# Attention stage of a hybrid block: TensorE's order written by the build's scheduler instead of by hand, with the value products marked urgent and taken in reverse

## The chip, the cores and the metric

The kernel runs on one core of one Trainium2 chip. The metric is the device time of one execution in microseconds (us), the median over the timed runs. The profile shows one further execution, taken by the hardware profiler. Its engines are named PE (TensorE matmul), PEld (TensorE weight load), DVE (VectorE), ACT (ScalarE), POOL (GpSimd) and SP (SyncE, which here issues the DMAs).

## The reference, cut to what matters

One layer over 2048 latent tokens and 256 context tokens of width 1024. After a modulated norm and one input projection, two head groups run on the same tokens: softmax attention and a gated recurrence. Their outputs are concatenated, projected, added to the stream, and a SwiGLU feed-forward follows.

```python
def block(q):                                   # one block of 128 queries; 8 heads, 2 key/value heads
    s = jnp.einsum('bqkgd,bnkd->bkgqn', q, keys).astype(jnp.float32) * scale
    p = jax.nn.softmax(s, axis=-1)              # over 2304 keys: 256 context, 2048 latent
    return jnp.einsum('bkgqn,bnkd->bqkgd', p.astype(vals.dtype), vals)

att_x = latent_attention(qx, kx, vx, kc, vc)
hg_x, hg_c = hgrn2_bidirectional(px[3:], pc[3:], lb_all[l], g_hg[l])     # 4 heads, both directions
x = x + mx[2] * (jnp.concatenate([att_x, hg_x], axis=-1) @ w_out[l])
x = x + mx[5] * swiglu(modulate(rmsnorm(x, g_norm2[l]), mx[3], mx[4]), w_gu[l], w_down[l])
return rmsnorm(x, g_final)
```

## The kernel before, in words

The program has five stages: the modulation vectors; the input projection; attention and recurrence together; the output projection with the second norm; the feed-forward. The change lies in the third, which works on TensorE with two independent streams of work.

**Attention.** The loop goes over 64 items: 2 key/value heads, 16 query blocks, and 2 pairs of query heads (`work`, L880). An object `Pair` holds one item. Its parts are:

- `scores(hh, i)` (L802): the scores of one head against all 2304 keys, in two pieces that live in two PSUM tiles, `s0` with 1536 keys (6 matmuls) and `s1` with 768 keys (4 matmuls). Each tile has one buffer. DVE takes the minimum of each piece (L819) and then of both (L821); the queries carry a minus sign, so this is the row maximum. Then ACT writes the exponentials of both pieces, `pr` (L825), which frees `s0` and `s1`.
- `transposes(k2)` (L829): for one key tile of 256 keys, four TensorE transposes (two blocks of 128 keys, two heads) into a PSUM tile `pt`, and one copy to `pf` in SBUF, by ACT (L840) or for three of the nine tiles by DVE (L838). A pair has 9 key tiles, and `pf` has 9 buffers.
- `products()` (L842): 18 calls, two for each key tile, that multiply `pf` with the values into one PSUM tile `av` (the profile shows 36 matmuls, since one of these calls becomes two instructions), and a copy `ot` by ACT (L851).
- `finish()` (L853): two transposes (`pof`, L862), the division by the row sum, and the store.

`pt`, `av` and `pof` share one PSUM pool of two buffers, `ps_t2`.

**Recurrence.** A generator `recurrence()` (L751) yields after each small step. It runs two units at a time; a unit is 512 tokens of one head. A unit has seven levels, and in each TensorE forms `pa` (four matmuls, L639), DVE merges it (L642), POOL multiplies four tensors (L651, L654, L663, L665) and ACT copies two (L657, L658); the next level's `pa` needs these. A unit also has `pd` (L628), transposes `pk` (L679) and state products `psf` and `psb` (L686, L698); each head ends with outputs `po` (L729 to L731). All TensorE results of the recurrence go through one PSUM buffer, `ps_h`.

**What sets the order.** The whole program is written as Python, and when it is built a scheduler writes one queue of instructions for each engine. It works along a modelled time line: whenever an engine is free in the model, it takes, of the instructions whose inputs and buffers are there in the model, the one that stands earliest in the Python program. The engines then run their queues in the order written. Inside `manual_schedule(engines={PE})` the scheduler keeps TensorE's instructions in the order of the Python program; the other engines' queues are still its own. The context named `border` (L895, L896) puts the whole third stage under that rule. Its order is this tuple, walked once for each item (L961):

```python
ORDER = (-1, 2, -2, 2, 0, 2, 0, 9, 1, 0, 0, -3, 2, -4, 0)
```

A negative number is a score piece of the current pair (head 0: -1 and -2; head 1: -3 and -4), a positive number is that many key tiles' transposes of the previous pair, 0 is some steps of the recurrence (`other()`), and 9 is the `finish` of the pair before that. The products of the previous pair follow at the end.

Of the kernel before, what the change touches and what calls it, by code (L numbers as in the profile page):

```python
# [57 lines left out]
def rows_bcast(ap, n=P):  # L58

    return bass.AP(tensor=ap.tensor, offset=ap.offset, ap=[[0, n], [1, ap.size()]])  # L60
# [12 lines left out]
def block_kernel(ctx: ExitStack, tc: tile.TileContext, a: dict, out: bass.AP, dbg=None):  # L73
    nc = tc.nc
# [3 lines left out]
    def pool(stack, name, bufs=1, space=None, side=None):  # L78
        kw = dict(name=name, bufs=bufs, reuse_waits="tile", side=side)
        if space is not None:  # L80
            kw["space"] = space
        return stack.enter_context(tc.tile_pool(**kw))
# [67 lines left out]
    with ExitStack() as st:  # L150
# [11 lines left out]
        for j in range(8):  # L162
            wm = wmp.tile([P, KT, 256], F32, tag="wm", name=f"wm{j}")
            nc.sync.dma_start(wm, w_mod_r[:, :, j * 256:(j + 1) * 256])
            if j in DVE_MOD:
                for r in range(2):
# [5 lines left out]
                    for i in range(2):  # L172
                        nc.tensor.matmul(pcol[:, 2 * j + i, r:r + 1], acc[:, i * P:(i + 1) * P], ones,
                                         start=True, stop=True)
                continue
            pm = ps_m.tile([P, 512], F32, tag="mm", name=f"pm{j}", bufs=2)
            for k in range(KT):
                nc.tensor.matmul(pm[:2, :256], sc[:, k, :], wm[:, k, :],
                                 start=(k == 0), stop=(k == KT - 1))
# [391 lines left out]
    with ExitStack() as st:  # L571
# [221 lines left out]
        class Pair:  # L793
# [48 lines left out]
            def products(self):  # L842

                av = ps_t2.tile([P, 512], F32, tag="t", name=f"av{self.nm}")[:, :256]
                for n, k2 in enumerate(T_ORDER):
                    for i in range(2):
                        nc.tensor.matmul(av[i * 64:(i + 1) * 64], self.kv[1][:, 2 * k2 + i, :],  # L847
                                         self.pf[k2][:, i * 256:(i + 1) * 256],
                                         start=(n == 0), stop=(n == len(T_ORDER) - 1))
                self.ot = op.tile([P, 256], F32, tag="ot", name=f"ot{self.nm}")  # L850
                nc.scalar.activation(self.ot, av, AF.Copy)  # L851

# [3 lines left out]
        T_ORDER = tuple(range(NKT // 2))  # L856
# [16 lines left out]
        def load_kv(g):  # L873
            kv = (kvp.tile([P, NTOK], F32R, tag="K", name=f"K{g}"),
                  kvp.tile([P, NTOK // P, 64], F32, tag="V", name=f"V{g}"))
            nc.sync.dma_start(f32v(kv[0]), s_k[g])
            nc.sync.dma_start(kv[1], s_v[:, g * 64:(g + 1) * 64].rearrange("(t p) v -> p t v", p=P))
            return kv
# [5 lines left out]
        def other():  # L884

            nonlocal rec, debt
            debt += STEPS / SLOTS
            while debt >= 1 and rec is not None:
                debt -= 1
                if next(rec, 0) == 0:  # L890
                    rec = None

        prev = done = None
        kv = None
        border = ExitStack()  # L895
        border.enter_context(tc.manual_schedule(engines={mybir.EngineType.PE}))  # L896
        for item in work + [None]:
            if item is None:
                while rec is not None:
                    other()  # L900
                order_T = iter(T_ORDER)
                for k2 in order_T:
                    prev.transposes(k2)
                    if done is not None:
                        done.finish()
                        done = None
                prev.products()
                prev.finish()
                border.close()
                hst.close()  # L910
                p5 = ctx.enter_context(ExitStack())
                wsp = pool(p5, "wsp", 3)
                wop = pool(p5, "wop")
                wo = [[wop.tile([P, D], F32R, name=f"wo{w}{k}") for w in "hl"] for k in range(KT)]
                gate1 = wop.tile([P, D], F32, name="gate1")
                mp = pool(p5, "mp", 2)
                ps_y = pool(p5, "ps_y", 2, PSUM)
                ps_mt = pool(p5, "ps_mt", 2, PSUM)
                for k in range(KT):
                    ws = wsp.tile([P, D], F32, tag="ws", name=f"wos{k}")  # L920
                    nc.sync.dma_start(ws, a["w_out"][0, k * P:(k + 1) * P, :])
                    nc.scalar.activation(wo[k][0], ws, AF.Copy)  # L922
                    (nc.vector if k in WOV else nc.gpsimd).tensor_tensor(  # L923
                        wo[k][1], ws, f32v(wo[k][0]), op=ALU.subtract)
                nc.sync.dma_start(gate1, rows_bcast(modrow[0, 2 * D:3 * D]))

                mixed = {}

                def mix_token(t):

                    rw = slice(t * P, (t + 1) * P)
                    mx = mp.tile([P, D], F32, tag="mix", name=f"mix{t}")
                    for g in range(2):
                        nc.sync.dma_start(mx[:, g * 256:(g + 1) * 256], s_att[g][rw, :])
                    for h in range(NH):
                        nc.sync.dma_start(mx[:, 512 + h * P:512 + (h + 1) * P], s_hg[h][rw, :])
                    mh = mp.tile([P, KT, P], F32R, tag="mh", name=f"mh{t}")
                    ml = mp.tile([P, KT, P], F32R, tag="ml", name=f"ml{t}")
                    for kk in range(2):
                        pt = ps_mt.tile([P, 512], F32, tag="t", name=f"mt{t}_{kk}")  # L940
                        for i in range(4):
                            k = kk * 4 + i
                            nc.tensor.transpose(pt[:, i * P:(i + 1) * P], mx[:, k * P:(k + 1) * P], ident)  # L943
                        pv = pt.rearrange("p (k t) -> p k t", t=P)
                        nc.scalar.activation(mh[:, kk * 4:kk * 4 + 4, :], pv, AF.Copy)
                        nc.vector.tensor_tensor(ml[:, kk * 4:kk * 4 + 4, :], pv,
                                                f32v(mh[:, kk * 4:kk * 4 + 4, :]), op=ALU.subtract)
                    mixed[t] = mh, ml

                mix_token(0)  # L950
                break
            qt, g, hp2 = item
            if (qt, hp2) == (0, 0):
                kv = load_kv(g)
            if hp2 == 0:
                qs = qpl.tile([P, 2, 2, 2, P], F32R, tag="qs", name=f"qs{qt}_{g}")
                nc.sync.dma_start(f32v(qs.rearrange("p h r a t -> p (h r a t)")),
                                  s_q[g][qt].rearrange("p h x -> p (h x)"))
            cur = Pair(item, kv, qs)
            todo = list(T_ORDER) if prev is not None else []  # L960
            for step in ORDER:  # L961
                if step < 0:
                    cur.scores((-step - 1) // NSEG, (-step - 1) % NSEG)
                elif step == 0:
                    other()
                elif step == 9:
                    if done is not None:
                        done.finish()
                else:
                    for _ in range(step):  # L970
                        if todo:
                            prev.transposes(todo.pop(0))
            if prev is not None:
                prev.products()
            prev, done = cur, prev
# [4 lines left out]
    with ExitStack() as st:  # L980
# [88 lines left out]
        for pair in (1, 0):  # L1069
# [9 lines left out]
            for ff in range(NFF):  # L1079
# [23 lines left out]
                for hf in range(2):  # L1103
                    pg = []
                    for ab in range(2):
                        p = ps_g.tile([P, 512], F32, tag="g", name=f"pg{nm}{hf}{ab}")
                        for k in range(KT):
                            for i, (wi, xi) in enumerate(((0, 0), (0, 1), (1, 0))):
                                nc.tensor.matmul(p, gws[ab][wi][:, k, :], h2[hf][xi][:, k, :],  # L1109
                                                 start=(k == 0 and i == 0),  # L1110
                                                 stop=(k == KT - 1 and i == 2))
# [19 lines left out]
                for j in range(8):  # L1131
# [5 lines left out]
                    for hf in range(2):  # L1137
# [5 lines left out]
                        for i, (l, r) in enumerate(mm):  # L1143
                            nc.tensor.matmul(pd, l[:, ts_], r[:, cs], start=(i == 0),  # L1144
                                             stop=(i == len(mm) - 1))
# [60 lines left out]
```

## Time and profile before

| what | us |
|---|---|
| timed runs | 3646.53, 3642.28, 3637.43 (median 3642.28) |
| the profiled execution, its own time | 3638.36 |
| its span, from the first to the last instruction | 3636.6 |
| PE busy in the span | 3473.4 (96%) |
| third stage, from its first to its last score matmul | 720.0 to 1932.8 |
| last recurrence output matmul starts | 1914.9 |
| last product matmul of the stage starts | 1970.6 |

Busy time is the time in which at least one instruction of the engine runs; matmuls are pipelined, so a busy PE is not PE at its peak. "Idle before" is the time an engine waited directly ahead of a group, and the arrow names what ended most of it. PEclk is the TensorE clock that was granted, as a share of full speed.

### The profile page before, as it was taken

The numbers are of one execution on the slowest core, as the hardware profiler recorded it, in microseconds if no ns is written. First come the engines' busy times: TensorE is split into PE (matmuls) and PEld (weight loads), VectorE is DVE, ScalarE is ACT, GpSimd is POOL, SyncE is SP. The second block draws the span as 40 slices with busy tenths as digits, with TensorE's granted clock in tenths as the row PEclk, the third lists the DMA queues.
The fourth block names the chain that finished last, engine by engine and source line by source line (L and its number), as shares of the span: only waits on it lengthen the run. The fifth ranks groups of instructions, "written<-read, shape, count | busy, mean of one in ns | idle before, by whom it ended". The sixth has DMA issues, their size and how long they took to land. (4 is left out here: it accounts for less than half of the span.)

```text
span 3636.6 us, 50114 instructions
## 1 busy us (share of the span) xinstructions
PE 3473.4 (96%) x19860; PEld 2870.8 (79%) x19860; DVE 1693.5 (47%) x2868; ACT 1251.8 (34%) x2299; POOL 1087.3 (30%) x1016
## 2 busy tenths in 40 slices
PE   8999999979899899899989999999999999999999
PEld 6999888967777777777777878888888888888887
DVE  6335654066655666566554552322323523223225
ACT  5322322166555656565643231111111211111112
POOL 4322222055324525434411132122122422221223
PEclk9999999989999999999999999999999999999999
DMA  7344655321121121011005451111111511111112
GB/s 237 95 133 146 176 175 154 95 65 35 32 61 33 33 72 39 30 45 39 22 21 168 152 184 53 41 58 47 41 52 55 213 57 47 47 52 41 53 46 87
DMA packets 279964, 293.94 MB, mean 81 GB/s; under 512 B 23120, under 2 KB 241200, under 8 KB 278448
## 3 DMA queue, kind: packets, MB, share of 16 engines
q1 hardware_dynamic: 279728, 290.73, 25.6%
q8 instruction: 156, 2.56, 0.3%
q14 instruction: 80, 0.66, 0.1%
HBM read 208.86 MB, written 81.81 MB: 80 GB/s over the span
## 5 line engine op out<-in xcount | busy, mean ns | idle before, releaser
L819 DVE TENSOR_REDUCE neg<-s 128x1 f32<-128x1536 f32 (+1 forms) x256 | 338.1, 1352 | 152.8 <-PE s L817 152.4
L1116 DVE TENSOR_TENSOR sa<-pg,sa 128x512 f32<-128x512 f32 x88 | 60.9, 692 | 682.5 <-PE pg L1109 668.0
L1089 POOL TENSOR_TENSOR gl<-gs,gh 128x1024 fp32r<-128x1024 f32 x88 | 211.8, 2407 | 500.4 <-ACT gh L1088 500.3
L817 PE MATMUL s<-K,qs 128*128 128x512 f32 (+1 forms) x1280 | 347.8, 403 | 6.8 <-ACT pr L825 5.4
L825 ACT ACTIVATE pr<-s,neg 128x1536 f32<-128x1536 f32 (+1 forms) x256 | 309.7, 1215 | 73.2 <-DVE neg L821 73.1
L834 PE MATMUL pt<-identr,pr 128*128 128x128 f32 x2304 | 316.2, 277 | 17.2 <-ACT pf L840 6.6
L1149 DVE TENSOR_TENSOR yy<-yy,pd 128x512 f32<-128x512 f32 x320 | 216.8, 685 | 207.6 <-PE pd L1144 207.0
L834 PEld LDWEIGHTS pt<-identr,pr 128*128 128x128 f32 x2304 | 265.2, 142 | 57.0 <-DVE pf L838 13.8
L840 ACT ACTIVATE pf<-pt 128x512 f32<-128x512 f32 x384 | 216.3, 596 | 213.9 <-PE pt L834 213.5
L817 PEld LDWEIGHTS s<-K,qs 128*128 128x128 f32 x1280 | 232.2, 198 | 68.7 <-ACT pr L825 14.3
L1109 PE MATMUL pg<-h2l,gh 128*128 128x512 f32 x704 | 279.1, 396 | 0.0
L1109 PE MATMUL pg<-h2lr,gh 128*128 128x512 f32 x704 | 279.1, 396 | 0.0
L1109 PE MATMUL pg<-h2h,gl 128*128 128x512 f32 x704 | 279.0, 397 | 0.0
L1109 PE MATMUL pg<-h2h,gh 128*128 128x512 f32 x704 | 279.0, 397 | 0.0
L1109 PE MATMUL pg<-h2hr,gl 128*128 128x512 f32 x704 | 279.0, 396 | 0.0
L1109 PE MATMUL pg<-h2hr,gh 128*128 128x512 f32 x704 | 279.0, 396 | 0.0
L1144 PE MATMUL pd<-dl,hh 128*128 128x512 f32 x704 | 274.4, 390 | 0.0
L1144 PE MATMUL pd<-dh,hl 128*128 128x512 f32 x704 | 274.3, 390 | 0.0
L1144 PE MATMUL pd<-dh,hh 128*128 128x512 f32 x704 | 274.2, 389 | 0.0
L847 PE MATMUL av<-pf,V 128*64 128x256 f32 x2304 | 262.8, 382 | 0.1
L1099 POOL TENSOR_TENSOR dl<-ds,dh 128x1024 fp32r<-128x1024 f32 x44 | 107.6, 2446 | 500.2 <-ACT dh L1098 495.3
L1098 ACT ACTIVATE dh<-ds 128x1024 fp32r<-128x1024 f32 x44 | 46.8, 1063 | 547.5 <-PE pd L1144 466.1
(248 smaller groups left out, 7437.5 us busy)
## 6 DMA issues: line engine op xcount, KB each, us to landing
gs<-in_w_gu_dram SPq DMA_DIRECT2D x88, 512.0 KB
wm<-in_w_mod_dram SPq DMA_DIRECT2D x24, 1024.0 KB
ds<-in_w_down_dram SPq DMA_DIRECT2D x44, 512.0 KB
s_q<-sq SPq DMA_DIRECT2D x128, 128.0 KB
qs<-s_q SPq DMA_DIRECT2D x32, 512.0 KB
ws<-in_w_in_dram SPq DMA_DIRECT2D x9, 1024.0 KB
xt<-in_x_dram SPq DMA_DIRECT2D x16, 512.0 KB
s_f<-ft SPq DMA_DIRECT2D x16, 512.0 KB
```

The lines of the kernel that those rows point to most:

```text
L817: nc.tensor.matmul(s[:, o - k0:o - k0 + w], self.qs[:, hh, self.item[2], half, :], self.kv[0][:, o:o + w], start=(half == 0), stop=(half = ...
L819: nc.vector.tensor_reduce(neg[:, i:i + 1], s[:, :n], axis=AX.X, op=ALU.min)
L825: nc.scalar.activation(pr[:, k0:k0 + n], self.s[j][:, :n], AF.Exp, bias=neg[:, NSEG:], scale=-1.0, accum_out=self.ls[:, hh, j:j + 1])
L834: nc.tensor.transpose(pt[:, (2 * i + hh) * P:(2 * i + hh + 1) * P], self.prs[hh][:, (2 * k2 + i) * P:(2 * k2 + i + 1) * P], ident)
L840: nc.scalar.activation(pf, pt, AF.Copy)
L847: nc.tensor.matmul(av[i * 64:(i + 1) * 64], self.kv[1][:, 2 * k2 + i, :], self.pf[k2][:, i * 256:(i + 1) * 256], start=(n == 0), stop=(n = ...
L1089: nc.gpsimd.tensor_tensor(wl, ws, f32v(wh), op=ALU.subtract)
L1099: nc.gpsimd.tensor_tensor(dl, ws, f32v(dh), op=ALU.subtract)
L1109: nc.tensor.matmul(p, gws[ab][wi][:, k, :], h2[hf][xi][:, k, :], start=(k == 0 and i == 0), stop=(k == KT - 1 and i == 2))
L1116: nc.vector.tensor_tensor(t, pg[1], t, op=ALU.mult)
L1144: nc.tensor.matmul(pd, l[:, ts_], r[:, cs], start=(i == 0), stop=(i == len(mm) - 1))
L1149: nc.vector.tensor_tensor(ys[j][:, cs], ys[j][:, cs], pd, op=ALU.add)
```

## The change

Three edits, all in the third stage. The `border` context goes, so TensorE's queue in this stage is written by the scheduler, with the Python order only as its preference. The product matmuls are issued inside `tc.high_priority()`, so that once they are ready the scheduler takes them ahead of everything else on TensorE. They go through the key tiles from the last to the first, `T_ORDER[::-1]`, so the first of them needs the key tile that was copied last. Nothing is computed otherwise: the same matmuls, copies, buffers and DMAs remain. (The score tiles are as before.)

```diff
             def products(self):
                 av = ps_t2.tile([P, 512], F32, tag="t", name=f"av{self.nm}")[:, :256]
-                for n, k2 in enumerate(T_ORDER):
-                    for i in range(2):
-                        nc.tensor.matmul(av[i * 64:(i + 1) * 64], self.kv[1][:, 2 * k2 + i, :],
-                                         self.pf[k2][:, i * 256:(i + 1) * 256],
-                                         start=(n == 0), stop=(n == len(T_ORDER) - 1))
+                with tc.high_priority():
+                    for n, k2 in enumerate(T_ORDER[::-1]):
+                        for i in range(2):
+                            nc.tensor.matmul(av[i * 64:(i + 1) * 64], self.kv[1][:, 2 * k2 + i, :],
+                                             self.pf[k2][:, i * 256:(i + 1) * 256],
+                                             start=(n == 0), stop=(n == len(T_ORDER) - 1))
                 self.ot = op.tile([P, 256], F32, tag="ot", name=f"ot{self.nm}")
                 nc.scalar.activation(self.ot, av, AF.Copy)
...
         prev = done = None
         kv = None
-        border = ExitStack()
-        border.enter_context(tc.manual_schedule(engines={mybir.EngineType.PE}))
         for item in work + [None]:
...
                 prev.products()
                 prev.finish()
-                border.close()
                 hst.close()
```

## The prediction

> **What bounds the kernel now.** I read the page first, then the busy times by stretch, then the groups of the third stage with what ended the idle time before them, then the timeline inside it.
>
> ```profile
> span 3636.6 us, 50114 instructions
> ...
> PE 3473.4 (96%) x19860; PEld 2870.8 (79%) x19860; DVE 1693.5 (47%) x2868; ACT 1251.8 (34%) x2299; POOL 1087.3 (30%) x1016
> ```
>
> ```profile
> 720.00:760.00 40.00, 20.37 (x112) 17.51 (x112) 25.88 (x42) 20.47 (x43) 25.15 (x29) 0.74 0.50 146
> 760.00:1915.00 1155.00, 1047.54 (x7524) 846.22 (x7525) 703.53 (x1160) 680.42 (x1301) 447.97 (x614) 0.97 0.13 38
> ...
> 2160.00:3636.00 1476.00, 1467.80 (x6335) 1190.42 (x6333) 501.97 (x604) 264.18 (x376) 377.74 (x171) 1.00 0.20 63
> ```
>
> The columns are the stretch, its length, the busy times of PE, PEld, DVE, ACT and POOL, the granted clock, and DMA. PE bounds the kernel, but not everywhere alike. In the feed-forward (last row) it is idle for 8 of 1476 us. In the attention stage it is busy 1047.54 of 1155 us, with DVE busy 703.53 and ACT 680.42, and in the 40 us that open the stage it is busy 20.37. Only this stage is changed, and only its idle PE time, near 127 us in these two rows, can be won. The groups say who waits; the last three columns are busy us, mean ns, and the idle us before them.
>
> ```profile
> L817 PE MATMUL s<-K,qs 128*128 128x512 f32 (+1 forms) x1280 | 347.8, 403 | 6.8 <-ACT pr L825 5.4 <-ACT ot L851 1.3
> ...
> L834 PE MATMUL pt<-identr,pr 128*128 128x128 f32 x2304 | 316.2, 277 | 17.2 <-ACT pf L840 6.6 <-DVE pf L838 4.9 <-ACT pr L825 2.4
> ...
> L847 PE MATMUL av<-pf,V 128*64 128x256 f32 x2304 | 262.8, 382 | 0.1
> ...
> L639 PE MATMUL pa<-Q,M 128*128 128x128 f32 x896 | 133.7, 294 | 43.8 <-POOL Q L665 17.0 <-DVE S L693 9.1 <-DVE A L642 7.3
> ...
> L729 PE MATMUL po<-V,A 128*128 128x128 f32 x128 | 27.1, 296 | 7.5 <-DVE o L746 5.6 <-DVE neg L821 1.8
> ...
> L862 PE MATMUL pof<-identr,ot 128*128 128x128 f32 x128 | 26.4, 288 | 7.8 <-DVE pf L838 7.7
> ...
> L698 PE MATMUL psb<-V,kt 128*128 128x128 f32 x144 | 22.8, 305 | 9.2 <-DVE S L693 6.4 <-DVE A L642 2.0 <-ACT dS L701 0.8
> ...
> L686 PE MATMUL psf<-V,kt 128*128 128x128 f32 x144 | 20.9, 287 | 9.0 <-ACT kt L681 3.2 <-ACT A L629 3.0 <-DVE A L642 1.6
> ...
> L628 PE MATMUL pd<-q,kk 128*128 128x128 f32 x128 | 19.4, 299 | 20.2 <-POOL kk L622 16.3 <-ACT kt L681 1.9 <-DVE A L642 1.2
> ...
> L679 PE MATMUL pk<-identr,C 128*128 128x128 f32 x72 | 18.6, 281 | 5.6 <-ACT kt L681 4.6 <-DVE A L642 1.0
> L679 PE MATMUL pk<-identr,M 128*128 128x128 f32 x72 | 18.5, 280 | 3.9 <-DVE A L642 2.7 <-ACT kt L681 1.2
> ```
>
> Idle before attention's groups: 6.8 + 17.2 + 0.1 + 7.8 = 31.9 us. Idle before the recurrence's (L639, L729, L698, L686, L628, L679): 43.8 + 7.5 + 9.2 + 9.0 + 20.2 + 5.6 + 3.9 = 99.2 us, of which 16.3 is one wait of L628. Together 131.1 us. The hand order's price is thus mostly the recurrence: TensorE stands at the head of its queue for POOL, DVE or ACT to finish a level, while attention's matmuls lie behind.
>
> **The change part by part.** The sum is made against the profiled execution, 3638.4 us (the span and 1.8 us around it); the median of the runs shown, 3642.3, lies 3.9 above it, and the forecast is given on the median.
>
> *The border goes.* No instruction is removed or added, no DMA moves by itself, and no engine does other work; only the order of TensorE's queue changes, and with it the times at which the others are fed. First what it can win. The one long wait opens the stage:
>
> ```profile
> 728.47 0.89 ACT L825 ACTIVATE pr<-s,neg 128x768 f32<-128x768 f32 x1
> ...
> 738.61 2.08 PE L628 MATMUL pd<-q,kk 128*128 128x128 f32 x8 [16.34 <-POOL kk L622]
> ...
> 740.34 2.86 PE L817 MATMUL s<-K,qs 128*128 128x512 f32 x10
> ```
>
> Columns: start, length, engine and instruction, and in brackets the idle time with its releaser. Head 1's score matmuls (third row) stand behind `pd` in the hand order. Their tile was free when the first exponential ended, which is where the second starts, 728.47. A free order issues them near 728.6, 11.7 us earlier. Next late is then the same head's chain through DVE and ACT, which no order shortens; I take **10 us won** (ends 0 and 16.3).
>
> The other recurrence waits are 99.2 - 16.3 = 82.9 us. A free order can put attention's work into them, but not always: in a lull of the score chain nothing of attention is ready. I take half, **41 us won** (ends 0 and 82.9). Of attention's own 31.9 us, waits for copies that free `pt` buffers remain unless a recurrence step happens to be ready; I take a third, **10 us** (ends 0 and 31.9). Sum of the gains 61 us, at most 131.
>
> Now what it can lose. A written order fits the machine as far as the modelled durations fit. In the hand order a level's `pa` comes several groups after its inputs were started; a scheduler that fills every gap puts it where the model says the inputs end, and whatever the chip takes longer, TensorE then waits at the head of its queue with everything else behind it. The longest such path between two `pa` is POOL's four multiplications:
>
> ```profile
> L663 POOL TENSOR_TENSOR Q<-Q,T x96: 615/659/899, 755.8 to 1846.7; 128x256 f32<-128x256 f32 x96
> ```
>
> ```profile
> L654 POOL TENSOR_TENSOR C<-M,T 128x256 f32<-128x256 f32 x96 | 67.9, 709 | 17.7 <-PE pk L679 8.2 <-ACT M L657 3.2 <-issue 2.1
> L651 POOL TENSOR_TENSOR M<-M,T 128x256 f32<-128x256 f32 x96 | 67.1, 699 | 34.3 <-PE pk L679 33.9
> L663 POOL TENSOR_TENSOR Q<-Q,T 128x256 f32<-128x256 f32 x96 | 66.6, 694 | 210.1 <-PE pa L639 209.9
> L665 POOL TENSOR_TENSOR Q<-Q,T 128x256 f32<-128x256 f32 x96 | 66.4, 692 | 0.0
> ```
>
> One shape takes 615 to 899 ns (minimum, median and maximum in the first row). I take as slip of a level the means over that minimum: 94 + 84 + 79 + 77 = 334 ns. There are 896 / 8 = 112 levels (a `pa` is four calls and shows as eight matmuls in the timeline): **37 us lost**. The ends: nothing, or a gain counted above, where the model is longer than the chip; and every operation at the slowest, 4 x (899 - 615) = 1136 ns a level, 127 us.
>
> A second loss: groups get cut up. The output projection lies outside the border, so its order is the scheduler's already, and it shows what a cut costs:
>
> ```profile
> 1956.35 0.39 PE L1001 MATMUL y<-woh,ml 128*128 128x512 f32 x1
> 1956.58 1.03 PE L834 MATMUL pt<-identr,pr 128*128 128x128 f32 x8
> 1957.37 0.48 PE L1001 MATMUL y<-woh,mh 128*128 128x512 f32 x1
> 1957.69 0.39 PE L1001 MATMUL y<-wol,mh 128*128 128x512 f32 x1
> 1957.92 0.40 PE L1001 MATMUL y<-woh,ml 128*128 128x512 f32 x1
> ```
>
> Start to start, two projection matmuls lie 0.23 us apart (last two rows); the first one after a set of transposes keeps its successor back 0.32. A change of kind costs 0.09 us. The hand order changes kind about as seldom as it can. I estimate ten more changes for each of 64 pairs (transposes taken one key tile at a time, recurrence steps between them): 640 x 0.09 = **58 us lost**. The ends: none, and one at each of the 20 score matmuls of a pair (1280 / 64), 115 us.
>
> *Products first.* Order among themselves is free (0.1 us idle before L847; every `pf` is there by then). Taking the last copied tile first means that `av` takes a buffer of `ps_t2` only when no transpose of its pair needs one; cost nothing, covered by that. The priority is not free. Here is how the products lie now:
>
> ```profile
> 1306.51 0.20 ACT L825 ACTIVATION_READ_ACCUMULATOR pr<-s,neg 128x1 f32 x1
> ...
> 1310.90 1.09 ACT L840 ACTIVATE pf<-pt 128x512 f32<-128x512 f32 x2 [1.27 <-PE pt L834]
> ...
> 1311.00 0.96 PE L817 MATMUL s<-K,qs 128*128 128x512 f32 x4
> ...
> 1311.88 4.11 PE L847 MATMUL av<-pf,V 128*64 128x256 f32 x36
> ...
> 1313.32 1.54 ACT L825 ACTIVATE pr<-s,neg 128x1536 f32<-128x1536 f32 x1 [1.33 <-DVE neg L821]
> ...
> 1315.92 1.65 PE L817 MATMUL s<-K,qs 128*128 128x512 f32 x6
> ```
>
> The piece `s1` goes first, then 4.11 us of products, and exactly in that time DVE and ACT turn the scores into exponentials, so that the next pair's scores start when the products end. If the products run ahead of that piece, the chain starts 4.1 us later and TensorE has for it only recurrence steps and a few early transposes. I put 0.8 us against that (the issue time of four score matmuls and a few transposes), so 3.3 us a pair are open, 64 x 3.3 = 211 us in the worst case. But the piece's buffer is free at 1306.7 (first row), while the last key tile's copy runs until 1312.0 (second row): the piece is ready well before the products. I take one pair in eight, **26 us lost**, ends 0 and 211.
>
> *Clock.* Stalls cost more than their length:
>
> ```profile
> 1907.00:1911.00 4.00, 1.01 (x6) 0.55 (x7) 2.32 (x6) 0.60 (x1) 1.43 (x2) 1.00 0.06 16
> 1911.00:1915.00 4.00, 3.98 (x24) 4.00 (x25) 0.00 (x0) 0.00 (x0) 1.27 (x1) 0.66 0.43 111
> ```
>
> PE was busy 1.01 of 4 us, and then the granted clock was 0.66 for 4 us, 1.4 us more lost. Over the 1155 us it was 0.97, 3% of 1047.5 or 31 us. I put none of it into the sum, since new stalls replace old ones; 31 us go into both ends.
> The Trainium skill, page "TensorE: Matmul & The Clock Gate", section "What's actually happening", says that the clock halves only after an idle window of about 3.4 us. By that rule the short stalls which the change removes or makes would leave the clock alone and the 31 us would stay lost in either order; the trace does not quite agree, as a clock of 0.66 followed a stretch that still held 1.01 us of matmuls.
>
> Sum: -61 + 37 + 58 + 26 = +60 us. On the median: **3702 us**. This likeliest case alone: from +15 (cuts 13 instead of 58) to +140 (slips 117 instead of 37, near their slow end), 3657 to 3782.
>
> **The rivals.** *The gaps fill and nothing slips.* TensorE always has something to take: the recurrence runs ahead, until POOL (447.97 of 1155 us busy) limits it. For it: DVE and ACT have room (61% and 59%), and the score chain leaves lulls that recurrence work fits. Against it: DVE and ACT would be close to full while the recurrence runs ahead, and once it is used up the lulls have nothing in them. Gains 61 us and half the clock's 31: 3642 - 76 = 3566. This decides if the model's times are no shorter than the chip's.
> *Products ahead of the last score piece in every pair.* For it: they now win whenever both are ready. Against it: the margin above. 211 - 61 = +150: 3792. It decides from the point where the last copy ends before the second exponential of head 0.
> *The order comes out as before.* The Python order is the scheduler's preference, and it is the hand order. Only the waits would be filled here and there, and the slips would take that back: 3642, within 11 us. Against it: the recurrence's steps, held back now by the queue (POOL waits for `pa`), are bound to move ahead.
>
> **How the numbers follow.** A measurement of this kernel tells about 0.3%, 11 us, from no change. Chances: forecast 0.44, products ahead 0.14, gaps fill 0.36, as before 0.06. Faster by over 0.3% is 0.36, within it 0.06, slower 0.58. The range must reach the filled gaps: their case spans some 3520 to 3631 (all 131 us, or little), and 3560 leaves out a third of it, 0.13; at the upper end 3800 leaves out 0.07. The forecast's own range is 3657 to 3782.
>
> **What would show it.** Right, if the idle time before `pa` (L639) and before the score matmuls grows over 43.8 and 6.8 us, with POOL and ACT as releasers; if the transposes' groups in the timeline are shorter and mixed with others; if the stretch from 760 to the last scores is longer than 1155 us. The opening wait of 16.3 us should be mostly gone in any case, and the recurrence's last outputs (now at 1914.9) should come earlier. Wrong, if PE's idle time in the stage falls below 100 us and the clock there rises from 0.97: then the gaps were filled. If the products start before the 4 score matmuls of the second piece in most pairs, it is the second rival.

## The result, and the profile after

| | us | ratio to the kernel before |
|---|---|---|
| kernel before | 3639.86 (3636.41 to 3646.53) | |
| changed kernel | 3679.07 (3675.97 to 3686.28) | 1.0108, 95% interval 1.0087 to 1.013 |
| its profiled execution | 3686.28, span 3684.5 | |

The change makes the kernel slower, by 39 us; 3702 was forecast. The direction and the range hold, but the sum behind them does not: as the experiments show, one edit alone (the border) gains 86 us, more than was put down for it, another (the reversal), costed at nothing, loses 125, and the third (the priority) does nothing.

From the page of the changed kernel, the span and the busy times:

```profile
span 3684.5 us, 50112 instructions
...
PE 3486.5 (95%) x19860; PEld 2855.9 (78%) x19860; DVE 1683.7 (46%) x2868; ACT 1247.5 (34%) x2299; POOL 1088.1 (30%) x1016
```

The profiled execution is 48 us longer than the one before. Of that, 12 us lie ahead of the stage: its first score matmul starts at 732.35 instead of 720.0, in a part that the change does not touch (in the runs below that start lies anywhere from 721.3 to 736.4). From there to the first matmul of the feed-forward it is 2202.8 - 732.4 = 1470.4 us, against 2156.3 - 720.0 = 1436.3 before: 34 us are the change's. Between the first product and the last the difference is 38 us, so the loss lies there. That stretch, by the busy times of stretches (the columns as in the prediction), in the kernel before and then in the changed one:

```profile
759.90:1971.00 1211.10, 1099.27 (x7847) 885.87 (x7846) 732.07 (x1198) 707.55 (x1344) 461.59 (x623) 0.97 0.15 44
```

```profile
774.90:2024.00 1249.10, 1113.23 (x7892) 874.74 (x7892) 723.71 (x1199) 703.44 (x1342) 465.58 (x627) 0.99 0.14 42
```

TensorE's idle time is length less busy time: 111.8 us before, 135.9 after. That is 24 of the 38 us; the other 14 are longer busy time. The groups of the changed kernel say what the idle time stood before:

```profile
L834 PE MATMUL pt<-identr,pr 128*128 128x128 f32 x2304 | 339.3, 281 | 64.9 <-DVE pf L838 31.0 <-ACT pf L840 26.0 <-DVE neg L821 5.9
L817 PE MATMUL s<-K,qs 128*128 128x512 f32 (+1 forms) x1280 | 329.2, 391 | 51.8 <-ACT pr L825 51.0
...
L849 PE MATMUL av<-pf,V 128*64 128x256 f32 x2304 | 264.4, 384 | 13.0 <-ACT pf L840 13.0
L639 PE MATMUL pa<-Q,M 128*128 128x128 f32 x896 | 131.2, 290 | 13.3 <-ACT dS L701 3.1 <-DVE A L642 2.9 <-POOL M L651 1.4
L864 PE MATMUL pof<-identr,ot 128*128 128x128 f32 x128 | 27.1, 294 | 4.9 <-DVE pf L838 4.4
L729 PE MATMUL po<-V,A 128*128 128x128 f32 x128 | 25.8, 284 | 0.2 <-ACT dS L701 0.2
L686 PE MATMUL psf<-V,kt 128*128 128x128 f32 x144 | 20.4, 283 | 0.5
L698 PE MATMUL psb<-V,kt 128*128 128x128 f32 x144 | 19.6, 277 | 0.1
...
L679 PE MATMUL pk<-identr,C 128*128 128x128 f32 x72 | 19.3, 291 | 0.1
L679 PE MATMUL pk<-identr,M 128*128 128x128 f32 x72 | 19.2, 291 | 5.3 <-DVE A L642 4.9 <-ACT kt L681 0.4
L628 PE MATMUL pd<-q,kk 128*128 128x128 f32 x128 | 17.5, 277 | 0.0
```

(L849 and L864 are the old L847 and L862.) The two streams changed places. The recurrence's waits fell from 99.2 us to 13.3 + 0.2 + 0.5 + 0.1 + 0.1 + 5.3 + 0.0 = 19.5. Attention's rose from 31.9 to 64.9 + 51.8 + 13.0 + 4.9 = 134.6. Waits of three sorts grew: scores for `pr` (the exponential that frees the score tile), transposes for `pf` (a copy that frees their PSUM buffer), and products for the last copy, a wait that was 0.1.

Two places show how. First the timeline of TensorE, ACT and DVE around one set of products:

```profile
1317.25 1.54 ACT L825 ACTIVATE pr<-s,neg 128x1536 f32<-128x1536 f32 x1
...
1318.93 1.66 PE L817 MATMUL s<-K,qs 128*128 128x512 f32 x6 [1.17 <-ACT pr L825]
...
1320.52 4.11 PE L849 MATMUL av<-pf,V 128*64 128x256 f32 x36
...
1324.96 0.94 PE L817 MATMUL s<-K,qs 128*128 128x512 f32 x4
...
1325.94 0.96 DVE L819 TENSOR_REDUCE neg<-s 128x1 f32<-128x768 f32 x1 [3.56 <-PE s L817]
```

The products stand between the 6 and the 4 matmuls of one head. The second piece's tile was free, but TensorE works on products for 4.11 us, and DVE is idle for 3.56 us before it gets the minimum on which both exponentials depend. In TensorE's queue as written this is so for 37 of 62 pairs; 21 more stand between the two heads, and 4 behind the whole score group, where the hand order has all of them.

The second place is the end of the stage, where the recurrence is used up:

```profile
1799.05 0.60 PE L834 MATMUL pt<-identr,pr 128*128 128x128 f32 x4
...
1799.68 0.60 ACT L840 ACTIVATE pf<-pt 128x512 f32<-128x512 f32 x1 [0.55 <-PE pt L834]
...
1800.33 4.11 PE L849 MATMUL av<-pf,V 128*64 128x256 f32 x36 [0.69 <-ACT pf L840]
```

The last tile is transposed, then copied, and only then can the first product start, since it needs just that tile: 1800.33 - 1799.05 = 1.28 us from transposes to products, 0.69 of it idle. This hole comes once in every pair. Recurrence steps can fill it while there are some, and they are used up sooner for it: the last recurrence output starts at 1727.5 instead of 1914.9.

### The profile page after: what moved, and what is told of

Its sections match the earlier page's. It is cut to its first block, busy times and chain, and to the rows that moved or that the text cites. A ratio compares the mean times of both kernels' runs of the same rounds, so it can differ in the third digit from the quotient of the medians.

```text
span 3684.5 us, 50112 instructions
## 1 busy us (share of the span) xinstructions
PE 3486.5 (95%) x19860; PEld 2855.9 (78%) x19860; DVE 1683.7 (46%) x2868; ACT 1247.5 (34%) x2299; POOL 1088.1 (30%) x1016
## 4 chain that ended last, share of the span: by engine, by line
PE 55%; DVE 3%; ACT 2%; issue 0%; DMA 0%; POOL 0%; SPq 0%; DVEq 0%; POOLq 0%; ACTq 0%
PE pg L1108 27%; PE pd L1143 13%; PE y L1000 5%; PE av L849 3%; PE s L817 3%; PE pt L834 2%; DVE neg L819 1%; DVE pf L838 1%; ACT pr L825 1%; ACT pf L840 1%; PE pa L639 1%; PE nt L1020 0%; PE mt L942 0%; DMA s_x<-x 0%; PE po L729 0%
## 5 line engine op out<-in xcount | busy, mean ns | idle before, releaser
L834 PE MATMUL pt<-identr,pr 128*128 128x128 f32 x2304 | 339.3, 281 | 64.9 <-DVE pf L838 31.0
L817 PE MATMUL s<-K,qs 128*128 128x512 f32 (+1 forms) x1280 | 329.2, 391 | 51.8 <-ACT pr L825 51.0
L825 ACT ACTIVATE pr<-s,neg 128x1536 f32<-128x1536 f32 (+1 forms) x256 | 312.1, 1222 | 62.8 <-DVE neg L821 57.1
L817 PEld LDWEIGHTS s<-K,qs 128*128 128x128 f32 x1280 | 227.0, 191 | 104.2 <-ACT pr L825 66.4
L840 ACT ACTIVATE pf<-pt 128x512 f32<-128x512 f32 x384 | 224.0, 596 | 185.2 <-PE pt L834 184.7
L849 PE MATMUL av<-pf,V 128*64 128x256 f32 x2304 | 264.4, 384 | 13.0 <-ACT pf L840 13.0
L849 PEld LDWEIGHTS av<-pf,V 128*64 128x64 f32 x2304 | 160.5, 137 | 103.8 <-ACT pf L840 17.5
```

The source lines that it names most:

```text
L817: nc.tensor.matmul(s[:, o - k0:o - k0 + w], self.qs[:, hh, self.item[2], half, :], self.kv[0][:, o:o + w], start=(half == 0), stop=(half = ...
L825: nc.scalar.activation(pr[:, k0:k0 + n], self.s[j][:, :n], AF.Exp, bias=neg[:, NSEG:], scale=-1.0, accum_out=self.ls[:, hh, j:j + 1])
L834: nc.tensor.transpose(pt[:, (2 * i + hh) * P:(2 * i + hh + 1) * P], self.prs[hh][:, (2 * k2 + i) * P:(2 * k2 + i + 1) * P], ident)
L840: nc.scalar.activation(pf, pt, AF.Copy)
```

## The experiments

Each ratio is to the kernel before, in runs on the same chip, with its 95% interval. In e3 to e7, e11 and e12 the helper that holds instructions back moves the lines of attention down by five: L822 is the old L817 (scores), L830 and L845 the old L825 and L840 (exponentials and copies), L854 the products.

**The reversal alone, in the hand order.** The changed kernel with the border put back:

```diff
+        border = ExitStack()
+        border.enter_context(tc.manual_schedule(engines={mybir.EngineType.PE}))
...
+                border.close()
```

> TensorE's order is written by hand as before; only the products take the key tiles last first. Theory R (the reversal itself costs, because the products' first matmul now waits for the copy that ends last, idle before L849 0.1 to 13.0 us in the changed kernel): +10 to +20 us, and most of the 39 us would need another cause. Theories P (the scores run a pair ahead and the products and transposes get into the score chain) and T (the recurrence runs ahead and leaves attention a tail without filler) both: within 5 us of the kernel before, since in the hand order four score matmuls and a finish lie between the last copy and the products. The prediction costed it at nothing.

3650.16 us, 1.0023 (1.001 to 1.0036): 8 us. Its group of products:

```profile
L849 PE MATMUL av<-pf,V 128*64 128x256 f32 x2304 | 265.8, 385 | 2.5 <-ACT pf L840 2.2
```

In the hand order four score matmuls and recurrence steps stand between the last copy and the products, so the hole is nearly covered. The 8 us lie in neither range, under R's and over that of P and T, and are a small part of the loss, which at this point left P and T.

**The recurrence ahead, in the hand order.**

```diff
-STEPS = 4.4
+STEPS = 5.7
```

> The kernel before with STEPS 5.7 for 4.4: the order stays written by hand, only the recurrence ends after 194 of the 256 score tiles, as in the changed kernel. Theory T (a tail without filler): attention alone needs 14.7 to 15.2 us a pair where its PE work is 12.5, so 16 pairs of tail leave some 2.2 to 2.7 us idle each: +35 to +43 us, as much as the whole change. Theory P: what the tail loses was PE work that the earlier pairs do, and they get it with fewer waits or not: within 15 us of the kernel before.

3698.7 us, 1.015 (1.0129 to 1.0172): 55 us, more than either theory had. Its size speaks for T, its mechanism does not. Two of its groups:

```profile
L639 PE MATMUL pa<-Q,M 128*128 128x128 f32 x896 | 138.5, 301 | 57.3 <-DVE S L693 15.7 <-DVE A L642 14.2 <-POOL Q L665 12.9
...
L679 PE MATMUL pk<-identr,M 128*128 128x128 f32 x72 | 19.4, 292 | 18.3 <-DVE neg L821 8.4 <-DVE A L642 5.5 <-DVE o L746 2.8
```

Most of the time went into the recurrence's own waits (57.3 for 43.8 before `pa`, 18.3 for 3.9 before `pk`): its steps follow each other more closely and TensorE stands at each. The recurrence's groups have 136.9 us of idle time before them for 99.2, attention's 34.2 for 31.9. The tail itself, behind the last recurrence output (1776.3) up to the last product, has little:

```profile
1778.00:2026.30 248.30, 232.05 (x1609) 174.87 (x1609) 137.29 (x205) 146.76 (x250) 19.20 (x22) 0.99 0.16 53
```

TensorE is idle there for 16 us, where T had put 35 to 43. So this run alone could not say what a run-ahead costs where TensorE may take something else; the next pair of runs and e5 do.

**Pacing the recurrence under the scheduler, and holding the products in step.** In e3 each recurrence step is queued behind the score matmul before it (`behind` wraps `tc.issue_after`, which puts what is written inside it later in the same engine's queue than the instruction named; here that is the latest matmul of a kind, `s` for scores and `av` for products):

```diff
                 elif step == 0:
-                    other()
+                    with behind("s"):
+                        other()
```

> The changed kernel, but each recurrence step is queued behind the score matmul that stands before it in the program, so that the recurrence ends after 252 of the 256 score tiles. The products stay free. Theory T: the tail is filled, 39 us come back and some of the filled waits besides: 3580 to 3640 us (0.983 to 1.00). Theory P: the products still stand between the two heads' scores or inside the second head's, the loss stays: 3660 to 3690 (1.005 to 1.014).

In e4 the recurrence is free, and products and scores were meant to stand to each other as in the hand order:

```diff
                 if step < 0:
-                    cur.scores((-step - 1) // NSEG, (-step - 1) % NSEG)
+                    with behind("av") if step == -1 else ExitStack():
+                        cur.scores((-step - 1) // NSEG, (-step - 1) % NSEG)
...
-                prev.products()
+                with behind("s"):
+                    prev.products()
```

> The changed kernel, but the products of a pair are queued behind the last score piece of the next pair, and a pair's first scores behind the products that stand before them, as the hand order has it. Transposes, finishes and the recurrence stay free; the recurrence ends after 217 of the 256 score tiles. Theory P: the score chain no longer has products in it, the loss goes: 3600 to 3645 us (0.989 to 1.001). Theory T: the tail is 10 pairs for 16, so 10/16 of the loss stays: +15 to +27 us, 3655 to 3667.

e3: 3628.29 us, 0.9957 (0.9945 to 0.9969). e4: 3645.61, 1.0001 (0.9989 to 1.0012). By their ratios both came out where T and P respectively had put them, and each takes away most of the loss, so neither decided. And e4 is not the test of P that it was meant to be. Its edit holds back only the first score piece of a pair (step -1). The second has a tile of its own, and in 25 of 62 pairs TensorE's queue has it ahead of the products, which then stand inside a head's scores after all:

```profile
1023.43 1.48 PE L822 MATMUL s<-K,qs 128*128 128x512 f32 x4
...
1026.03 4.11 PE L854 MATMUL av<-pf,V 128*64 128x256 f32 x36 [0.47 <-ACT pf L845]
1030.07 1.66 PE L822 MATMUL s<-K,qs 128*128 128x512 f32 x6
```

I turned T into theory C (crowding), and tried both constraints at once and the pace by itself.

**The pace by itself, under the scheduler.** The paced kernel with one number changed.

```diff
-STEPS = 4.4
+STEPS = 5.7
```

> The paced kernel with one number changed: STEPS 5.7 for 4.4. The recurrence's steps stay queued behind the score matmul that stands before them, but there are more of them for each pair, and the recurrence ends after 196 of the 256 score tiles (252 in the paced kernel, 194 in the changed one). Theory C (crowding: the earlier the recurrence is done, the more of its work lies between attention's steps on DVE and ACT, and the longer the stretch without filler behind it): +30 to +55 us on the kernel before, 3674 to 3700. Rival (the paced kernel's gain comes from the queueing itself and not from the pace): 3620 to 3640, as the paced kernel.

3629.63 us, 0.995 (0.9933 to 0.9968), the same as the paced kernel. C falls: with the scheduler's order it does not matter that the recurrence is done early. What the constraint changed is something else, and in TensorE's queue as written only one thing stood out: the products split a head's scores in 12 pairs here and in 6 in e3, against 37.

**Both constraints.** The edits of e3 and e4 together.

> Both constraints: products behind the next pair's last score piece, that pair's first scores behind the products before them, and the recurrence's steps behind the score matmul before them (it ends after 252 score tiles). Only the transposes and the finishes are left to the scheduler. Theory P (products inside the score chain cost): 3600 to 3620 us, below the paced kernel's 3628. Theory C alone (where the products stand matters little once the recurrence is paced): 3622 to 3640.

3658.44 us, 1.0032 (1.0022 to 1.0042), slower than either, and above both ranges. It says less against P than it seems to: like e4's, its edit holds back only the first score piece of a pair, and in 16 of 62 pairs products stand inside a head's scores, in e3 in 6. Its products:

```profile
L854 PE MATMUL av<-pf,V 128*64 128x256 f32 x2304 | 272.0, 391 | 33.8 <-ACT pf L845 33.5
```

They wait 33.8 us, nearly all for the last copy, more than in any other run. With nearly everything else held in its place there is less left to put into the hole; this reading was not tested by itself. That pointed to the reversal.

**The products forward again.** In e7 the paced kernel takes the tiles as they are copied (the edit shown); e8 is the kernel before with only the border gone.

```diff
-                    for n, k2 in enumerate(T_ORDER[::-1]):
+                    for n, k2 in enumerate(T_ORDER):
```

> The paced kernel with the products taking the key tiles in the order in which they are copied, first one first. Theory R (the reversal makes the products wait for the last copy: 8.2 us idle before them in the paced kernel, and +8 us measured in the hand order): 5 to 10 us below the paced kernel, 3618 to 3624. Rival (the products' groups now get cut, 77 groups for 62, and more changes of kind, 934 for 890, take it back): 3626 to 3636.

> The changed kernel without the products' edits: the order is left to the scheduler, the products are as before (first copied tile first, no priority). By its order the recurrence ends after 251 of the 256 score tiles, products stand between the two heads' scores in 53 of 62 pairs, and TensorE changes kind 961 times (883 before). Theory C (the run-ahead of the recurrence is the cost, and it comes with the reversal): 3610 to 3640 us, not slower than the kernel before. Theory P (products inside the score chain): 3655 to 3680. The prediction's own terms (slips of the recurrence, cut groups): 3655 or more as well.

e7: 3566.05 us, 0.9778 (0.9756 to 0.98), by the ratios (0.9957 - 0.9778) x 3642 = 65 below the paced kernel where 5 to 10 were expected. e8: 3562.72 us, 0.9765 (0.9745 to 0.9785), below every range that was put down for it. So leaving TensorE's order to the scheduler gains 86 us, and the products' edits lose (1.0108 - 0.9765) x 3642 = 125. All of that is the reversal's: without the priority the changed kernel builds to the same program, instruction for instruction. The stretch from the first product to the last in e8:

```profile
774.20:1903.80 1129.60, 1075.21 (x7873) 867.39 (x7872) 714.64 (x1198) 705.98 (x1350) 469.49 (x632) 0.99 0.16 47
```

Idle 54.4 us for 111.8 in the kernel before, and 24 us less busy time at a clock of 0.99 for 0.97. Three of its groups:

```profile
L834 PE MATMUL pt<-identr,pr 128*128 128x128 f32 x2304 | 330.5, 278 | 37.7 <-DVE pf L838 22.7 <-ACT pf L840 11.7 <-DVE neg L821 1.8
L817 PE MATMUL s<-K,qs 128*128 128x512 f32 (+1 forms) x1280 | 323.5, 389 | 20.8 <-ACT pr L825 20.2 <-DMA K<-s_k 0.3
...
L639 PE MATMUL pa<-Q,M 128*128 128x128 f32 x896 | 130.2, 287 | 6.9 <-POOL Q L665 3.0 <-DVE A L642 2.3 <-DVE S L693 0.5
```

With its smaller groups the recurrence's waits come to 10.1 us (99.2 before) and attention's to 62.0 (31.9 before).

**What in the reversal costs.** Either the buffer of `pf` that the next pair's first copy wants is freed last (M1), or no product can start before the last copy (M2). Two orders separate these:

```diff
-                    for n, k2 in enumerate(T_ORDER[::-1]):
+                    for n, k2 in enumerate((8,) + T_ORDER[:8]):            # e9
+                    for n, k2 in enumerate(T_ORDER[:8][::-1] + (8,)):      # e10
```

> The changed kernel with the products' order 8, 0, 1, ... 7 for 8, 7, ... 0: the key tile that is copied last still comes first, but the buffers of pf (9, as many as a pair has) come free in the order in which the next pair's copies want them. Theory M1 (the reversal costs because the buffer wanted first is freed last): the loss goes, 3555 to 3590 us. Theory M2 (it costs because no product may begin before the last copy ends, which leaves a hole of a copy's length for every pair): as the changed kernel, 3670 to 3690.

> The changed kernel with the products' order 7, 6, ... 0, 8: still reversed, and the buffers come free nearly as late as in the changed kernel, but the key tile that is copied last comes last. Theory M2: the other eight products run while that tile is transposed and copied, the loss goes, 3555 to 3580 us, as with the products untouched (3562.7). Theory M1: 3660 to 3690.

e9: 3686.26 us, 1.012 (1.0101 to 1.0139). e10: 3558.05 us, 0.9761 (0.9746 to 0.9777). M2, on both counts: one tile moved from first to last takes the whole loss away, with the other eight still reversed. The timeline of e10:

```profile
1329.48 0.94 PE L817 MATMUL s<-K,qs 128*128 128x512 f32 x4
...
1331.22 0.60 PE L834 MATMUL pt<-identr,pr 128*128 128x128 f32 x4
...
1331.75 4.11 PE L849 MATMUL av<-pf,V 128*64 128x256 f32 x36
...
1332.03 0.57 ACT L840 ACTIVATE pf<-pt 128x512 f32<-128x512 f32 x1
```

The last tile's copy (last row) runs beneath the first products. From its transposes to the products it is 1331.75 - 1331.22 = 0.53 us, for 1.28 at the place shown of the changed kernel. And the products follow the 4 matmuls of the second piece here; they do not split the head.

**How much of the loss is the split.** The second head's scores are queued behind the products that stand before them, with the reversal kept (e11), and with the products forward (e12):

```diff
                 if step < 0:
-                    cur.scores((-step - 1) // NSEG, (-step - 1) % NSEG)
+                    with behind("av") if step == -3 else ExitStack():
+                        cur.scores((-step - 1) // NSEG, (-step - 1) % NSEG)
```

> The changed kernel with one constraint: a pair's second head's scores are queued behind the products that stand before them in the program, so that products no longer come between the two score pieces of one head (1 of 62 for 37 of 62; 61 stand between the two heads). The reversal stays, and the recurrence ends after 228 score tiles. Theory P' (of the changed kernel's loss against the untouched products, some 57 us are products that split a head's scores, the rest the hole before the products): 3615 to 3640 us. Rival (the place of the products is indifferent, only the hole counts): 3665 to 3685.

> The same constraint with the products taking the tiles in the order of the copies: a version meant to be the fastest. Against the untouched products under the scheduler (3562.7 us), products that split a head's scores go from 6 of 62 to none, and changes of kind from 961 to 937. Theory P': 3550 to 3563 us. Rival (nothing is left there): 3560 to 3575.

e11: 3611.79 us, 0.9915 (0.9902 to 0.9928), a little below the expected 3615 to 3640. e12: 3570.53 us, 0.98 (0.9785 to 0.9815): no gain over e8, its rival was right. Of e11:

```profile
L822 PE MATMUL s<-K,qs 128*128 128x512 f32 (+1 forms) x1280 | 319.0, 388 | 24.5 <-ACT pr L830 24.1 <-DMA K<-s_k 0.4
L854 PE MATMUL av<-pf,V 128*64 128x256 f32 x2304 | 264.1, 383 | 22.7 <-ACT pf L845 22.7
```

The scores' wait for the exponentials is halved (51.8 to 24.5), the products' wait for the last copy is not (13.0 to 22.7). With this constraint 1.0108 becomes 0.9915, so (0.0193 x 3642) 70 us go with the split heads. The reversal under the same constraint costs 0.9915 - 0.98, 42 us. The other 13 of the 125 us are what the constraint itself costs (e12 against e8), so 70 is a little low for the split. The hole read off above, 1.28 - 0.53 = 0.75 us, times 64 pairs is 48 us, an estimate of what it costs where nothing fills it; of the 42 us, 20 show as idle time before the products (22.7 in e11, 2.9 in e12).

The runs with the last copied tile first under the scheduler agree with the split as the larger part. Their ratios follow the number of pairs with products inside a head: 1 (e11, 0.9915), 6 (e3, 0.9957), 12 (e5, 0.995), 16 (e6, 1.0032), 25 (e4, 1.0001), 37 (the changed kernel, 1.0108, and e9, 1.012), with only e6 and e4 clearly in reverse order.

## Why the prediction was right or wrong

*The step that failed* is "Order among themselves is free (0.1 us idle before L847; every `pf` is there by then)", with "cost nothing, covered by that". The row was read rightly, but it is a row of the hand order, in which four score matmuls and recurrence steps separate the last copy from the products. The first edit takes that cover away, and the prediction did not ask what the reversal costs without it. With the cover 8 us were lost (e1), without it 125 (e8 against the changed kernel). Two sorts of loss were missed: the hole of 0.75 us a pair (42 us by e11 and e12), and what the scheduler makes of products that get ready later, namely that they land inside a head's scores (70 us by e11). The priority, to which the prediction gave its one cost for the products ("The priority is not free"), changes nothing in this kernel.

*Gains.* Forecast 61, measured 86 for the border alone (e8). From the first product to the last its idle time falls by 57 us and its busy time by 24, with the clock at 0.99 for 0.97. So the idle time won is near the forecast, and what the sum lacks is mainly the clock, of which it took nothing. That the idle time is near is partly luck: the recurrence's waits, opening included, were put at 51 us won and fell by 89, attention's were put at 10 won and rose by 30. (In the changed kernel they fell by 79.7 and rose by 103.) The opening gave nothing: from the first score to the first product it is 774.9 - 732.4 = 42.5 us, 39.9 before. The wait before `pd` is gone as forecast, and "Next late is then the same head's chain through DVE and ACT" was right, but that chain grew, since DVE now works on the recurrence's first tensors and masks (`T`, L670, and L592) around the second head's minimum:

```profile
746.00:754.00 8.00, 0.00 (x0) 0.00 (x0) 8.00 (x11) 2.13 (x5) 8.00 (x9) 0.70 0.69 188
754.00:757.00 3.00, 2.57 (x6) 2.04 (x7) 2.90 (x5) 2.10 (x7) 3.00 (x4) 0.50 0.02 5
```

DVE and POOL are busy for all of the first 8 us, in which TensorE has nothing. (In e8 the opening takes 774.2 - 736.4 = 37.8 us, 2 less than before.)

*POOL slip, 37 us.* Not seen: the wait before `pa`, forecast to grow, fell from 43.8 to 13.3 and no longer names `Q` first (in e8 it is 6.9). Steps taken as soon as they are ready did not leave TensorE standing. The idle time before the scores grew as forecast (6.8 to 51.8, ACT as releaser), but from the score chain and not from slips.

*Groups cut up, 58 us.* Mis-sized: in the queue as written TensorE changes kind 930 times in this stage for 883. That is 47 and not 640, 4 us at 0.09 each. e8 changes kind 961 times and is among the fastest.

*Products ahead of the last score piece, 26 us.* The mechanism is there, the count was wrong (58 of 62 pairs and not one in eight), and the cause is not the priority: without it, e8 has 53 of 62. The second rival ("in every pair", 3792) named the place rightly and the time not: its price of 3.3 us a pair was too high. In TensorE's queue the scores have run ahead by a pair when the products come, which the price did not reckon with. Being ahead of the whole second head costs nothing that shows (53 of 62 pairs in e8, 3562.72, and in e12, 3570.53); being inside a head does.

*The first rival, gaps fill* (3566, half the clock's loss won), is the border alone, 3562.72. With the products' edits its own test gives a split answer: the clock rose to 0.99, the idle time rose as well.

So 3702 is near 3679 by luck: losses from three terms that hardly exist or were mis-sized (121 us) stood where one missed term of 125 belongs. The rest of the miss is the gains, which were 25 us too small, 24 of them busy time.

## What to carry to other kernels

An idle time of zero before a group is a property of the order around it, so when a change frees that order, ask of every "covered" edit what the cover was made of. Accumulate first what was produced first: the item that is ready last should come last in a chain, so that its copy runs beneath the others; here one tile moved from first to last was worth 3.5% once no fixed order hid it. And when a scheduler may reorder, find out where a long group (here 4.11 us of products) lands in the latency chain that feeds the other engines: between two chains no cost showed, within one it cost some 70 us over 37 pairs.

The best versions leave TensorE's order to the scheduler with the copied-last tile last: e10 (0.9761), e8 (0.9765) and e7 (0.9778), not to be told apart, all faster than either kernel. It stays open by which of its choices the scheduler puts reversed products within a head; that it is the late start was shown (e9, e10), the path from there to the place was not. It also stays open why the kernel with both constraints (e6) is slower than either alone. It has more split heads than e3 but fewer than e4, and the largest wait for the last copy; what each costs there was not separated.

## What the runs showed of the hardware

The clock follows the few microseconds in which TensorE is mostly idle, not the sum of idle time. After 8 us without a matmul it was 0.50 for 3 us (second row of the fence on the opening), yet in the changed kernel's stretch with 135.9 us of idle time it was 0.99, where the kernel before had 0.97 with 111.8. Counted from the traces, the changed kernel has ten gaps over 1.5 us in that stretch, together 21 us, and the kernel before 19, together 37 us. The Trainium skill, page "TensorE: Matmul & The Clock Gate", section "What's actually happening", ties the halved clock to an idle window of about 3.4 us; the 8 us gap agrees with it, but the kernel before does not. The longest gap in its stretch is 2.97 us, and behind it the clock was halved:

```profile
1490.90:1493.80 2.90, 0.00 (x0) 0.00 (x0) 0.73 (x1) 0.84 (x2) 2.90 (x5) 0.76 0.10 28
1493.80:1499.20 5.40, 5.35 (x19) 4.67 (x20) 3.15 (x4) 0.90 (x2) 4.33 (x6) 0.50 0.01 2
```

The prediction left the clock out of its sum because new stalls replace old ones. By these rows short stalls do not replace long ones, and with the border gone and the products as before (e8) the clock does count: 0.99 for 0.97 on some 1099 us of busy time is about 22 us, an estimate, beside the 24 us by which the busy time fell.
